# Four of sixteen query tiles as rounded products of split operands

## The chip, the cores and the metric

The kernel runs on one core of one Trainium2 chip. TensorE multiplies, VectorE and ScalarE work element by element, GpSimd and SyncE mostly issue DMA transfers. The metric is the time of one execution on the device in microseconds (us). The kernel before took 2002.85 us (median of three runs, 2001.03 to 2003.95).

## The reference, cut to what matters

One decoder layer for 256 prompt tokens and 8 sample tokens, 264 in all, with 2048 channels in float32: input projection, a recurrent and an attention group, output projection, layer norm, and then a retrieval of experts. The change lies at the start of that retrieval, in `q` and what follows from it:

```
q  = jnp.dot(xb, wq).reshape(n, PEER_HEADS, 2, PEER_HALF)      # 2048 x 2048 weights
s1 = jnp.einsum('nhd,hkd->nhk', q[:, :, 0], sub_k1)
s2 = jnp.einsum('nhd,hkd->nhk', q[:, :, 1], sub_k2)
v1, i1 = lax.top_k(s1, PEER_TOPK)
v2, i2 = lax.top_k(s2, PEER_TOPK)
comb = v1[..., :, None] + v2[..., None, :]
sv, si = lax.top_k(comb.reshape(n, PEER_HEADS, -1), PEER_TOPK)
e = take(i1, si // PEER_TOPK) * N_KEYS + take(i2, si % PEER_TOPK)
g = softmax(sv)
act = gelu(einsum(xb, u_tab[e]));  out = einsum(g * act, v_tab[e])
```

## The kernel before

**Two ways of multiplying.** A float32 matrix product is done in one of two ways. The native one (`native`, line 940) hands TensorE plain float32 operands. The rounded one splits both operands into a high part, rounded to the type float32r, and a low part, which is the rest, and adds three products: high by high, high by low, low by high. The weights are split on their way: `split1_` (lines 103 and 106) lets ScalarE copy the high half of a raw tile of 1024 columns, and VectorE subtract it from the raw tile. The split halves lie in a ring of five pairs of tiles; raw weights come by DMA, issued by SyncE, into a ring of six half tiles, so three tiles of weights are there or on their way.

**The query tiles.** After the first layer norm, `x1` (named M in the rows) holds 264 tokens as columns, in 16 chunks of 128 channels. There are 16 tiles of 128 query channels, counted m = 0 to 15, each a native product over the 16 chunks. Tiles 0 and 1 (`first`) run while the layer norm still finishes. From m = 2 on a loop issues, in this order: the load of the weights two tiles ahead, the product of tile m, for an even m the scores of head m/2 − 1 (`scores`), and the eviction of tile m (`queries`: a copy by ScalarE of 256 columns into qT, and one of 8 into QS).

**Scores and top 16.** `scores` multiplies the two query tiles of a head with its keys on TensorE; ScalarE copies the result into one of three tiles SC, and VectorE runs `both`: the 16 largest of each half, then the 16 largest sums. After every second head `pick` follows on VectorE, for both halves of the tokens.

**The split of x1.** The products that follow the query tiles are of the expert table and need only the first 214 tokens; they are mostly rounded and read `x1s`, the split of these 214 columns of `x1`. It is made in the loop, two chunks a tile, for m = 2 to 9, by one copy (ScalarE) and one subtraction (VectorE) a chunk.

**What sets the order.** Nothing is moved by a scheduler in this part: each engine takes its instructions in the order in which the program writes them, and waits at one that is not ready with everything behind it. Only DMA queues run apart. After the loop `early` issues tiles of the expert table, the last picks and the gates; from `GSTART` on, transposes on TensorE of what the picks and gates gave (`tokens`).

Of the kernel before, what the change touches and what calls it, by code (L numbers as in the profile page):

```python
# [10 lines left out]
F32R = mybir.dt.float32r  # L11
# [3 lines left out]
OP = mybir.AluOpType  # L15
# [3 lines left out]
NC_ = 16  # L19
SEQ = 256  # L20
NB = 8
T = SEQ + NB
NPG = 8
NG = 50
ND = T - NG
# [16 lines left out]
TABT = 20  # L42

RUN = 34
NAT = 6
PICK = 1
GATE = 3
# [13 lines left out]
def _build(tc, I, O):  # L61
    nc = tc.nc
    ctx = ExitStack()
    PS = bass.MemoryType.PSUM
    with ctx:
        def pool_in(c, name, bufs, side=None):
            return c.enter_context(tc.tile_pool(name=name, bufs=bufs, side=side, reuse_waits="tile"))

        const = pool_in(ctx, "const", 1)
        big = pool_in(ctx, "big", 1)  # L70
# [22 lines left out]
        def halves(src):  # L93
            return [half(src[:, a:a + 8]) for a in (0, 8)]
# [20 lines left out]
        def pmm(shape=(128, T)):  # L115
            return psum.tile(list(shape), F32, name="mm", bufs=mmb[0])
# [51 lines left out]
        for a in range(0, NC_, 4):  # L168
            for i, j in enumerate(seq[:3]):
                if a % 8 == 0:  # L170
                    first[j].append(slots[2 * i + a // 8]())
                hi, lo = [t[:, a % 8:a % 8 + 4] for t in first[j][-1]]
# [527 lines left out]
        x1, wo = x0, {}  # L700
# [24 lines left out]
        QS = x0w[:, :NB * 260]  # L725
# [47 lines left out]
        for u in range(2 * NC_):  # L773
# [3 lines left out]
            if u % 2 == 0:  # L777
# [3 lines left out]
                hi, lo = wo.pop(u // 2)  # L781
# [3 lines left out]
            p = pmm()  # L785
            for i in range(4):
                k, x = u % 2 * 4 + i, mixes[0][:, u // NC_ * 4 + i]
# [14 lines left out]
        def load_u(k):  # L802

            ups[k] = halves(I["wq"][k + 16] if k < 0 else I["uT"][k])

        def split1(d, k, i, eng=None):
            d[k][i] = split1_(d[k][i], eng)
# [11 lines left out]
        def split2(k, eng=None):  # L819
            split1(ups, k, 0, eng)  # L820
            split1(ups, k, 1, eng)
# [86 lines left out]
        for c in range(NC_ + 1):  # L908
# [5 lines left out]
            if c < NC_:  # L914
                p = pm[c] = pmm()
                w = [None, wo.pop(NC_ + c)]
# [16 lines left out]
        ln.squares(15)  # L933
        ln.stats(2)

        x1s = big.tile([128, NC_, 2, ND], F32R, name="A")
        first = [(ups.pop(k), pmm()) for k in (-16, -15)]

        def native(p, w, c, n=T):
            nc.tensor.matmul(p, w[c // 8][:, c % 8, :], x1[:, c, :n], start=c == 0, stop=c == NC_ - 1)  # L940
# [104 lines left out]
        QS = qp.tile([128, 16, 64], F32, name="QS", bufs=1)  # L1045
        nc.gpsimd.memset(QS, 0.0)
        qT = {}

        def queries(m, p):
            h = m // 2  # L1050
            if m % 2 == 0:
                qT[h] = qp.tile([128, 2, SEQ], F32, name="qT")
            nc.scalar.copy(qT[h][:, m % 2, :], p[:, :SEQ])
            nc.scalar.copy(QS[:, m, h * 8:(h + 1) * 8], p[:, SEQ:])

        def scores(h):
            q = qT.pop(h)
            ps = pmisc([128, 2, 2, 128])
            for tt in range(2):
                for f in range(2):  # L1060
                    nc.tensor.matmul(ps[:, tt, f, :], q[:, f, tt * 128:(tt + 1) * 128], kk[:, 2 * h + f, :],
                                     start=True, stop=True)
            sc = qp.tile([128, 2, 2, 128], F32, name="SC", bufs=3)
            nc.scalar.copy(sc, ps)
            both(tops, [sc[:, tt] for tt in range(2)], h)
            if h % 2 and h < 7:
                for t in tops:
                    t.pick(h - 1, 2)

        def rows_out(a):  # L1070

            p = pmisc([NG, 512])
            for c in range(4):
                nc.tensor.transpose(p[:, c * 128:(c + 1) * 128], x1[:, a * 4 + c, ND:T], ident)
            xg = qp.tile([NG, 512], F32, name="xg", bufs=1)
            nc.scalar.copy(xg, p)
            nc.gpsimd.dma_start(xgd[:, a * 512:(a + 1) * 512], xg)

        load_u(-13)
        for m, (w, p) in enumerate(first):  # L1080
            queries(m, p)
        for m in range(2, 16):
            k = m - 16
            load_u(k + 2)
            w = ups.pop(k)
            p = pmm()
            for i in range(NC_):
                native(p, w, i)
            if m % 2 == 0:
                scores(m // 2 - 1)  # L1090
            queries(m, p)
            if m < 10:

                for c in range(2 * (m - 2), 2 * (m - 2) + 2):
                    nc.scalar.copy(x1s[:, c, 0], x1[:, c, :ND])
                    nc.vector.tensor_tensor(x1s[:, c, 1], x1[:, c, :ND], x1s[:, c, 0], op=OP.subtract)
            elif m < 14:
                rows_out(m - 10)

        def sample_scores():  # L1100
# [86 lines left out]
        def load_v(k):  # L1187
            downs[k] = []
            for a in (0, 4):
                raw = stream.tile([128, 8, 128], F32, name="raw")  # L1190
                nc.sync.dma_start(raw, I["vt"][k][:, 2 * a:2 * a + 8])
                downs[k].append(raw)

        def up(k, a=0, b=NC_):
            w = ups[k]
            if a == 0:
                pu[k] = pmm([128, 2, ND])
            p = pu[k]
            if k < NAT:
                for c in range(a, b):  # L1200
                    native(p[:, 0], w, c, ND)
                return
            for c in range(a, b):
                hi, lo = w[c // 8]
                nc.tensor.matmul(p, hi[:, c % 8, :], x1s[:, c], start=c == 0, stop=False)  # L1205
                nc.tensor.matmul(p[:, 0, :], lo[:, c % 8, :], x1s[:, c, 0], start=False, stop=c == NC_ - 1)  # L1206

        def act_sum(k):
            p = pu.pop(k)
            acts[k] = ex.tile([128, NE], F32, name="ac", bufs=RUN - 8)  # L1210
            nc.gpsimd.memset(acts[k][:, ND:], 0.0)
            ac = acts[k][:, :ND]
            if k < NAT:
                nc.scalar.activation(ac, p[:, 0], AF.Gelu_apprx_tanh)
                return
            nc.scalar.copy(ac, p[:, 1, :])
            nc.vector.tensor_tensor(ac, ac, p[:, 0, :], op=OP.add)

        def act_gelu(k):
            if NAT <= k and k in acts:  # L1220
                ac = acts[k][:, :ND]
                nc.scalar.activation(ac, ac, AF.Gelu_apprx_tanh)
# [5 lines left out]
        def gate_mult(k):  # L1228
            g, i = divmod(k, 8)
            ac = acts[k]  # L1230
            nc.vector.tensor_tensor(ac.rearrange("p (b t) -> p b t", t=16), ac.rearrange("p (b t) -> p b t", t=16),  # L1231
                                    gts[g].rearrange("p (b i t) -> p b i t", i=8, t=16)[:, :, i, :], op=OP.mult)
            W[k] = epool[0].tile([128, 2, ND], F32R, name="w", bufs=17)
            nc.scalar.copy(W[k][:, 0], ac[:, :ND])  # L1234
# [24 lines left out]
        def step(s):  # L1259
            v = s - RUN  # L1260
            k = v + 9
            if s >= 128:
                return last_step(v, k)
            if s + 2 < 128:
                load_u(s + 2)
            if v >= -2:
                load_v(v + 2)
            if k + LEAD >= 0 and (k + LEAD) % 8 == 0:
                load_g((k + LEAD) // 8)
            up(s)  # L1270
            if v >= 0:
                split1(downs, v, 0)
                if v >= 1:
                    add(v - 1)
                split1(downs, v, 1)
            if s - 1 in pu:
                act_sum(s - 1)
            d, n = (ups, s + 1) if s + 1 < 128 else (downs, v + 1)
            high(d, n, 0)
            if k >= 0:  # L1280
                gate_mult(k)
            if s != RUN:
                act_gelu(s - 1)
            low(d, n, 0)
            if k >= 0:
                gate_low(k)
            split1(d, n, 1)
            if v >= 0:
                down(v)

        def last_step(v, k):
# [3 lines left out]
            for n in (v + 2, v + 3):  # L1295
                if n < 128 and n not in downs:
                    load_v(n)
            if v + RUN == 128:
                act_sum(127)
# [15 lines left out]
        def early(s, gen):  # L1315

            load_u(s + 2)
            if s + 1 >= NAT:
                split2(s + 1)
# [10 lines left out]
            if s == GATE:  # L1330
                for t in tops:
                    t.less()
                for t in tops:
                    t.gate()
            if NAT <= s < NAT + 8:
                for c in range(2 * (s - NAT), 2 * (s - NAT) + 2):

# [13 lines left out]
        gen = gates()  # L1351
        for s in range(GSTART, RUN - 9 - LEAD):
            early(s, gen)
# [3 lines left out]
        epool.append(pool_in(ctx, "exw", 2))  # L1357
        act_gelu(RUN - 12 - LEAD)
        act_gelu(RUN - 11 - LEAD)
# [224 lines left out]
```

## Time and profile before

| what | us |
|---|---|
| median of three runs | 2002.85 |
| lowest, highest | 2001.03, 2003.95 |
| the profiled execution: its time | 2001.45 |
| the profiled execution: its span | 1999.6 |
| TensorE busy in the span | 1931.7 (97%) |
| VectorE busy | 1623.9 (81%) |
| ScalarE busy | 964.2 (48%) |

All rows below come from the profiled execution; times in them count from the start of its span. "Busy" is the time in which an engine had an instruction under way. TensorE's matmuls overlap in its pipeline: the time between two starts, not the length of one, is what a matmul costs in a stream. A native float32 matmul shows as two records. The names on both sides of the arrow are the program's tiles: mm and misc lie in PSUM, A is `x1s`, hi, lo, xl and sometimes A are the halves of split weights, SC the score tiles, qT and QS the queries, sip, vp, combp, eqp, sfp, sap and r1p tiles of the top 16 and the picks.

### The profile page before, as it was taken

The numbers are of one execution on the slowest core, as the hardware profiler recorded it, in microseconds if no ns is written. First come the engines' busy times: TensorE is split into PE (matmuls) and PEld (weight loads), VectorE is DVE, ScalarE is ACT, GpSimd is POOL, SyncE is SP. The second block draws the span as 40 slices with busy tenths as digits, with TensorE's granted clock in tenths as the row PEclk, the third lists the DMA queues.
The fourth block names the chain that finished last, engine by engine and source line by source line (L and its number), as shares of the span: only waits on it lengthen the run. The fifth ranks groups of instructions, "written<-read, shape, count | busy, mean of one in ns | idle before, by whom it ended". The sixth has DMA issues, their size and how long they took to land.

```text
span 1999.6 us, 37148 instructions
## 1 busy us (share of the span) xinstructions
PE 1931.7 (97%) x13906; PEld 1834.9 (92%) x13906; DVE 1623.9 (81%) x2961; ACT 964.2 (48%) x1601; POOL 405.0 (20%) x461
## 2 busy tenths in 40 slices
PE   8999899999899999999999999999999999999995
PEld 8888778798789999999999999999999999999995
DVE  6534756785599889679999999899999996989977
ACT  4223655643211898555455445554455443544443
POOL 2000000004000000113333333233333330321012
PEclk9999999999999999999999999999999999999997
DMA  9899599854344578779999999899999995998851
GB/s 314 285 370 332 188 328 320 285 175 150 109 144 137 187 233 273 258 260 377 352 332 349 350 333 353 319 337 353 333 349 351 331 351 183 378 332 306 285 189 54
DMA packets 182260, 562.09 MB, mean 281 GB/s; under 512 B 20514, under 2 KB 49278, under 8 KB 181698
## 3 DMA queue, kind: packets, MB, share of 16 engines
q1 hardware_dynamic: 148656, 447.96, 63.1%
q0 software_dynamic: 32560, 111.70, 15.9%
q8 instruction: 109, 1.79, 0.4%
q14 instruction: 71, 0.58, 0.1%
q10 hardware_dynamic: 864, 0.06, 0.0%
HBM read 540.03 MB, written 19.61 MB: 280 GB/s over the span
## 4 chain that ended last, share of the span: by engine, by line
PE 82%; DVE 6%; DMA 6%; ACT 4%; issue 1%; SPq 1%; POOL 0%; POOLq 0%; ACTq 0%; DVEq 0%
PE acc L1249 21%; PE mm L1205 18%; PE acc L1251 10%; PE mm L1206 9%; PE mm L940 8%; PE mm L302 3%; PE mm L304 2%; PE mm L303 2%; DMA cv<-in_ck 2%; DMA cv<-in_cv 2%; DVE lo L106 1%; PE acc L1153 1%; PE acc L642 1%; PE acc L563 1%; PE misc L381 1%
## 5 line engine op out<-in xcount | busy, mean ns | idle before, releaser
L106 DVE TENSOR_TENSOR lo<-raw,hi 128x1024 fp32r<-128x1024 f32 x273 | 332.9, 1222 | 76.6 <-ACT hi L103 76.4
L1249 PE MATMUL acc<-w,hi 128*128 128x428 f32 x1224 | 387.2, 373 | 0.0
L1205 PE MATMUL mm<-A,hi 128*128 128x428 f32 x1176 | 369.2, 372 | 0.0
L103 ACT CAST hi<-raw 128x1024 fp32r<-128x1024 f32 x273 | 284.3, 1045 | 171.4 <-PE acc L1249 81.1
L1251 PE MATMUL acc<-w,lo 128*128 128x214 f32 x1224 | 321.0, 262 | 4.0 <-DVE lo L106 4.0
L1206 PE MATMUL mm<-A,lo 128*128 128x214 f32 x1176 | 308.0, 262 | 3.3 <-DVE lo L106 3.3
L1249 PE MATMUL acc<-w,xl 128*128 128x428 f32 x824 | 261.4, 371 | 0.0
L1205 PE MATMUL mm<-A,xl 128*128 128x428 f32 x776 | 242.6, 371 | 0.0
L1251 PEld LDWEIGHTS acc<-w,lo 128*128 128x128 f32 x1224 | 235.2, 192 | 4.4 <-DVE lo L106 4.3
L1249 PEld LDWEIGHTS acc<-w,hi 128*128 128x128 f32 x1224 | 231.3, 189 | 8.6
L1206 PEld LDWEIGHTS mm<-A,lo 128*128 128x128 f32 x1176 | 226.3, 192 | 3.6 <-DVE lo L106 3.6
L1205 PEld LDWEIGHTS mm<-A,hi 128*128 128x128 f32 x1176 | 222.4, 189 | 6.9
L1402 POOL DMA_INDIRECT ug<-in_u,eix x102 | 152.2, 1492 | 334.7 <-DVE ug L1420 254.9
L1251 PE MATMUL acc<-w,xl 128*128 128x214 f32 x824 | 216.4, 263 | 0.0
L1402 POOL DMA_INDIRECT ug<-in_v,eix x102 | 145.8, 1429 | 339.7 <-DVE xrep L1434 279.3
L1206 PE MATMUL mm<-A,xl 128*128 128x214 f32 x776 | 202.5, 261 | 0.0
L103 ACT CAST xl<-raw 128x1024 fp32r<-128x1024 f32 x139 | 143.2, 1046 | 101.3 <-PE acc L1249 81.4
L1257 DVE TENSOR_TENSOR M<-M,acc 128x428 f32<-128x428 f32 x256 | 153.5, 600 | 41.3 <-PE acc L1251 36.8
L106 DVE TENSOR_TENSOR xl<-raw,xl 128x1024 fp32r<-128x1024 f32 x139 | 170.5, 1229 | 15.3 <-ACT xl L103 15.3
L1234 ACT CAST w<-ac 128x214 fp32r<-128x214 f32 x128 | 47.7, 373 | 277.4 <-DVE ac L1231 277.4
L1249 PEld LDWEIGHTS acc<-w,xl 128*128 128x128 f32 x824 | 155.5, 189 | 5.6
L940 PE MATMUL mm<-M,raw 128*128 128x264 f32 (+1 forms) x704 | 152.8, 378 | 6.7 <-ACT M L901 6.7
(382 smaller groups left out, 4053.3 us busy)
## 6 DMA issues: line engine op xcount, KB each, us to landing
raw<-in_uT SPq DMA_DIRECT2D x256, 512.0 KB
raw<-in_vt SPq DMA_DIRECT2D x256, 512.0 KB
raw<-in_w_in SPq DMA_DIRECT2D x74, 512.0 KB
cv<-in_ck SPq DMA_DIRECT2D x64, 512.0 KB
cv<-in_cv SPq DMA_DIRECT2D x64, 512.0 KB
raw<-in_wq SPq DMA_DIRECT2D x32, 512.0 KB
Gd<-stage SPq DMA_DIRECT2D x14, 1024.0 KB
gt<-Gd SPq DMA_DIRECT2D x16, 896.0 KB
```

Source lines behind the costliest of these rows:

```text
L103: nc.scalar.copy(hi, raw)
L106: (eng or nc.vector).tensor_tensor(lo, raw, hi, op=OP.subtract)
L302: nc.tensor.matmul(p, hi, xh[:, c], start=c == 0, stop=False)
L303: nc.tensor.matmul(p, hi, xl[:, c], start=False, stop=False)
L940: nc.tensor.matmul(p, w[c // 8][:, c % 8, :], x1[:, c, :n], start=c == 0, stop=c == NC_ - 1)
L1205: nc.tensor.matmul(p, hi[:, c % 8, :], x1s[:, c], start=c == 0, stop=False)
L1206: nc.tensor.matmul(p[:, 0, :], lo[:, c % 8, :], x1s[:, c, 0], start=False, stop=c == NC_ - 1)
L1234: nc.scalar.copy(W[k][:, 0], ac[:, :ND])
L1249: nc.tensor.matmul(p[:, c, :2 * ND].rearrange("p (b t) -> p b t", b=2), hi[:, b % 8, :], w, start=i == 0, stop=False)
L1251: nc.tensor.matmul(p[:, c, :ND], lo[:, b % 8, :], w[:, 0], start=False, stop=i == 7)
L1257: nc.vector.tensor_tensor(a, a, p[:, :, b * ND:(b + 1) * ND], op=OP.add)
L1402: nc.gpsimd.indirect_dma_start(out=t, out_offset=None, in_=tab, in_offset=bass.IndirectOffsetOnAxis(ap=eix[:, a, j:j + 1], axis=0))
```

## The change

Tiles m = 4, 5, 6 and 7 (`QR`) become rounded products. Four things follow in the program:

- `x1s` now holds the high and the low part of all 264 tokens, 528 columns a chunk, in another order: high of the last 50 tokens, high of the first 214, low of the first 214, low of the last 50. So the 428 columns that the expert products read stay next to each other. `split_x1` makes it at m = 2, all 16 chunks at once, with two copies and two subtractions a chunk; the split in the loop is gone.
- At m = 3 to 6 the weights of the next tile are split (`split2`: two copies on ScalarE, two subtractions on VectorE) before the product of tile m is issued.
- Each of the four products writes 314 columns of PSUM: the first and third matmul of a chunk add into columns 0 to 263, the second (high weights by low tokens) into columns 50 to 313.
- The eviction of such a tile is three copies by ScalarE (214, 42 and 8 columns) and two additions by VectorE (42 and 8 columns), which bring the shifted parts together.

```diff
+QR = (4, 5, 6, 7)
...
-        x1s = big.tile([128, NC_, 2, ND], F32R, name="A")
+        x1s = big.tile([128, NC_, 2 * T], F32R, name="A")
+        LO = T
...
+            if m in QR:
+                a, b = qT[h][:, m % 2, :], QS[:, m, h * 8:(h + 1) * 8]
+                nc.scalar.copy(a[:, :ND], p[:, NG:T])
+                nc.scalar.copy(a[:, ND:], p[:, T:T + NG - NB])
+                nc.scalar.copy(b, p[:, T + NG - NB:T + NG])
+                nc.vector.tensor_tensor(a[:, ND:], a[:, ND:], p[:, :NG - NB], op=OP.add)
+                nc.vector.tensor_tensor(b, b, p[:, NG - NB:NG], op=OP.add)
+                return
             nc.scalar.copy(qT[h][:, m % 2, :], p[:, :SEQ])
             nc.scalar.copy(QS[:, m, h * 8:(h + 1) * 8], p[:, SEQ:])
...
+        def split_x1():
+            for c in range(NC_):
+                for a, b, t in ((0, NG, slice(ND, T)), (NG, T, slice(0, ND))):
+                    nc.scalar.copy(x1s[:, c, a:b], x1[:, c, t])
+                nc.vector.tensor_tensor(x1s[:, c, LO:LO + ND], x1[:, c, :ND], x1s[:, c, NG:T], op=OP.subtract)
+                nc.vector.tensor_tensor(x1s[:, c, LO + ND:], x1[:, c, ND:], x1s[:, c, :NG], op=OP.subtract)
...
-            p = pmm()
+            if m == 2:
+                split_x1()
+            if m + 1 in QR:
+                split2(k + 1)
+            p = pmm((128, T + NG) if m in QR else (128, T))
             for i in range(NC_):
-                native(p, w, i)
+                if m not in QR:
+                    native(p, w, i)
+                    continue
+                hi, lo = w[i // 8]
+                nc.tensor.matmul(p[:, :T], hi[:, i % 8, :], x1s[:, i, :T], start=i == 0, stop=False, ...)
+                nc.tensor.matmul(p[:, NG:], hi[:, i % 8, :], x1s[:, i, LO:], start=False, stop=False, ...)
+                nc.tensor.matmul(p[:, :T], lo[:, i % 8, :], x1s[:, i, :T], start=False, stop=i == NC_ - 1, ...)
             if m % 2 == 0:
                 scores(m // 2 - 1)
             queries(m, p)
-            if m < 10:
-                for c in range(2 * (m - 2), 2 * (m - 2) + 2):
-                    nc.scalar.copy(x1s[:, c, 0], x1[:, c, :ND])
-                    nc.vector.tensor_tensor(x1s[:, c, 1], x1[:, c, :ND], x1s[:, c, 0], op=OP.subtract)
-            elif m < 14:
+            if 10 <= m < 14:
                 rows_out(m - 10)
```

The expert products (`up`) read the same 428 columns of `x1s` under new indices.

What stands where now. First VectorE, between the end of the top 16 of scores 0 (MAX_INDEX sip) and the start of the top 16 of scores 1 (MAX vp of SC). Before:

```order
L975 MAX_INDEX sip_7112<-svp_7111,combp_7192 128x8
L975 MAX_INDEX sip_7118<-svp_7117,combp_7195 128x8
L1096 TENSOR_TENSOR A<-M,A 128x214 x4
L967 MAX vp_7269<-SC 128x8 x2
L967 MAX vp_7271<-SC 128x8 x2
```

and with the change, where `lo<-raw,hi` and `xl<-raw,xl` are the low halves of the weights of tiles 4 and 5:

```order
L978 MAX_INDEX sip_7112<-svp_7111,combp_7256 128x8
L978 MAX_INDEX sip_7118<-svp_7117,combp_7259 128x8
L107 TENSOR_TENSOR lo<-raw,hi 128x1024
L107 TENSOR_TENSOR xl<-raw,xl 128x1024 x2
L107 TENSOR_TENSOR lo<-raw,hi 128x1024
L970 MAX vp_7369<-SC 128x8 x2
L970 MAX vp_7371<-SC 128x8 x2
```

The subtractions of x1 have gone from here, and the low halves of two whole weight tiles stand between the two top 16.

Second VectorE, between the end of the picks after scores 1 (TENSOR_REDUCE r1p) and the top 16 of scores 2. Before:

```order
L1018 TENSOR_TENSOR eqp_7333<-eqp_7333,xfp_7116 128x512
L1019 TENSOR_REDUCE r1p_7121<-eqp_7333 128x32
L1096 TENSOR_TENSOR A<-M,A 128x214 x4
L967 MAX vp_7399<-SC 128x8 x2
L967 MAX vp_7401<-SC 128x8 x2
```

and with the change:

```order
L1021 TENSOR_TENSOR eqp_7433<-eqp_7433,xfp_7116 128x512
L1022 TENSOR_REDUCE r1p_7121<-eqp_7433 128x32
L1061 TENSOR_TENSOR qT<-qT,mm 128x42
L1062 TENSOR_TENSOR QS<-QS,mm 128x8
L107 TENSOR_TENSOR lo<-raw,hi 128x1024 x2
L1061 TENSOR_TENSOR qT<-qT,mm 128x42
L1062 TENSOR_TENSOR QS<-QS,mm 128x8
L107 TENSOR_TENSOR xl<-raw,xl 128x1024 x2
L970 MAX vp_7573<-SC 128x8 x2
L970 MAX vp_7575<-SC 128x8 x2
```

Behind the picks stand now the additions of tile 4 (qT, QS), the low halves of tile 6, the additions of tile 5 and the low halves of tile 7.

Third TensorE, from the end of tile 2 through scores 0 (misc from kk and qT). Before:

```order
L940 MATMUL mm<-M,raw 128x264 x48
L1061 MATMUL misc<-kk,qT 128x128 x4
L940 MATMUL mm<-M,raw 128x264 x32
L1061 MATMUL misc<-kk,qT 128x128 x4
L940 MATMUL mm<-M,raw 128x264 x32
```

and with the change:

```order
L943 MATMUL mm<-M,raw 128x264 x48
L1072 MATMUL misc<-kk,qT 128x128 x4
L943 MATMUL mm<-M,raw 128x264 x16
L1115 MATMUL mm<-A,hi 128x264
L1116 MATMUL mm<-A,hi 128x264
L1117 MATMUL mm<-A,lo 128x264
L1115 MATMUL mm<-A,hi 128x264
L1116 MATMUL mm<-A,hi 128x264
L1117 MATMUL mm<-A,lo 128x264
```

Tile 3 is native as before; tile 4 starts with two products of the high half, and its third matmul reads the low half `lo`, as does every third one behind it.

## Rows read from the trace of the kernel before

**Rows 1.** The page's busy times (us, share, instructions), then one of its groups.

```profile
PE 1931.7 (97%) x13906; PEld 1834.9 (92%) x13906; DVE 1623.9 (81%) x2961; ACT 964.2 (48%) x1601; POOL 405.0 (20%) x461
...
L103 ACT CAST hi<-raw 128x1024 fp32r<-128x1024 f32 x273 | 284.3, 1045 | 171.4 <-PE acc L1249 81.1
```

**Rows 2.** Windows: length, busy time by engine (instructions), granted clock, DMA share, GB/s.

```profile
545.00:575.00 30.00, 30.00 (x145) 25.89 (x144) 29.20 (x130) 4.62 (x19) 0.00 (x0) 1.00 0.42 140
...
575.00:605.00 30.00, 30.00 (x145) 25.77 (x144) 29.45 (x132) 4.76 (x16) 1.08 (x2) 1.00 0.46 147
...
700.00:750.00 50.00, 48.01 (x357) 46.64 (x356) 44.14 (x114) 46.85 (x111) 1.42 (x10) 1.00 0.75 233
...
750.00:800.00 50.00, 46.69 (x343) 45.82 (x342) 45.67 (x130) 41.73 (x87) 0.00 (x0) 0.99 0.87 274
```

**Rows 3.** TensorE's timeline of the query tiles: start, us, engine, line, operation, records.

```profile
529.31 14.41 PE L940 MATMUL mm<-M,raw 128*128 128x264 f32 x64
...
543.55 1.05 PE L1061 MATMUL misc<-kk,qT 128*128 128x128 f32 x8
...
544.44 14.41 PE L940 MATMUL mm<-M,raw 128*128 128x264 f32 x64
...
573.82 1.05 PE L1061 MATMUL misc<-kk,qT 128*128 128x128 f32 x8
```

**Rows 4.** VectorE's timeline there; in brackets the idle time before, and its end.

```profile
530.13 0.87 DVE L967 MAX8 vp<-SC 128x8 f32<-128x128 f32 x4 [16.97 <-ACT SC L1064]
...
539.33 1.23 DVE L1096 TENSOR_TENSOR A<-M,A 128x214 fp32r<-128x214 f32 x4
...
545.26 0.87 DVE L967 MAX8 vp<-SC 128x8 f32<-128x128 f32 x4 [4.70 <-ACT SC L1064]
...
564.35 1.25 DVE L1096 TENSOR_TENSOR A<-M,A 128x214 fp32r<-128x214 f32 x4
```

**Rows 5.** TensorE's timeline of an input projection tile, three products a chunk.

```profile
19.72 0.28 PE L302 MATMUL mm<-xh,A 128*128 128x264 f32 x1
...
22.86 0.29 PE L304 MATMUL mm<-xh,lo 128*128 128x264 f32 x1
```

**Rows 6.** VectorE's timeline: the low halves of one weight tile.

```profile
665.63 1.23 DVE L106 TENSOR_TENSOR lo<-raw,hi 128x1024 fp32r<-128x1024 f32 x1 [1.18 <-ACT hi L103]
...
666.78 1.22 DVE L106 TENSOR_TENSOR xl<-raw,xl 128x1024 fp32r<-128x1024 f32 x1
```

**Rows 7.** ScalarE's timeline of the query tiles.

```profile
521.32 0.17 ACT L1054 COPY QS<-mm 128x8 f32<-128x8 f32 x1
...
521.50 0.37 ACT L1053 COPY qT<-mm 128x256 f32<-128x256 f32 x1
...
529.51 0.59 ACT L1064 COPY SC<-misc 128x512 f32<-128x512 f32 x1 [7.57 <-PE misc L1061]
...
530.31 0.66 ACT L1095 CAST A<-M 128x214 fp32r<-128x214 f32 x2
```

**Rows 8.** TensorE behind a wait: its timeline, then windows (busy, granted clock, DMA).

```profile
399.70 0.56 PE L788 MATMUL mm<-A,hi 128*128 128x264 f32 x1 [1.94 <-ACT A L281]
...
400.06 0.43 PE L789 MATMUL mm<-A,hi 128*128 128x264 f32 x1
...
402.26 0.42 PE L790 MATMUL mm<-A,lo 128*128 128x264 f32 x1
...
400.00:401.00 1.00, 1.00 (x6) 0.50 0.70 278
...
403.00:404.00 1.00, 1.00 (x10) 0.98 0.63 172
```

**Rows 9.** VectorE's last gate, and TensorE's first token transpose.

```profile
657.55 0.29 DVE L1032 TENSOR_TENSOR gp<-gp,zsp 128x128 f32<-128x128 f32 x1
...
659.75 0.27 PE L1115 MATMUL misc<-c_ident,r0p 128*128 128x128 f32 x1
```

**Rows 10.** VectorE's timeline: an operation on 32 columns.

```profile
554.47 0.15 DVE L1011 TENSOR_SCALAR sap<-sip 128x32 uint32<-128x32 uint32 x1
```

More of the change, by code (lines that the diff above doesn't have):

```diff
@@ L1085, in _build @@
             w = ups.pop(k)
-            p = pmm()
-            for i in range(NC_):
-                native(p, w, i)
+            if m == 2:
[3 more added lines that the diff above has]
+            p = pmm((128, T + NG) if m in QR else (128, T))
+            for i in range(NC_):
+                if m not in QR:
+                    native(p, w, i)
+                    continue
+                hi, lo = w[i // 8]
+                nc.tensor.matmul(p[:, :T], hi[:, i % 8, :], x1s[:, i, :T], start=i == 0, stop=False, skip_group_check=True)
+                nc.tensor.matmul(p[:, NG:], hi[:, i % 8, :], x1s[:, i, LO:], start=False, stop=False, skip_group_check=True)
+                nc.tensor.matmul(p[:, :T], lo[:, i % 8, :], x1s[:, i, :T], start=False, stop=i == NC_ - 1,
+                                 skip_group_check=True)
             if m % 2 == 0:
@@ L1204, in up @@
                 hi, lo = w[c // 8]
-                nc.tensor.matmul(p, hi[:, c % 8, :], x1s[:, c], start=c == 0, stop=False)
-                nc.tensor.matmul(p[:, 0, :], lo[:, c % 8, :], x1s[:, c, 0], start=False, stop=c == NC_ - 1)
+                nc.tensor.matmul(p, hi[:, c % 8, :], x1s[:, c, NG:NG + 2 * ND].rearrange("p (b t) -> p b t", b=2), start=c == 0, stop=False)
+                nc.tensor.matmul(p[:, 0, :], lo[:, c % 8, :], x1s[:, c, NG:T], start=False, stop=c == NC_ - 1)
         def act_sum(k):
```

## The prediction

> **What bounds the kernel now.** I read the busy times first, then a table of windows around the query tiles, then the timelines of TensorE, VectorE and ScalarE there. TensorE is busy 97% of the span and VectorE 81% [rows 1]; such a share hides which stage is whose. The windows show it: from 545 to 575 us TensorE is busy for all 30.00 us, and VectorE for 29.20 of them [rows 2]. So TensorE sets the pace while the query tiles run, but VectorE has almost nothing left there. Two query tiles without the scores between them take 14.24 us on TensorE (529.31 to 543.55), 7.12 each, and the scores 0.89 [rows 3]. Below, tile m is the m-th of the 16, counted from 0; "query tiles 5 to 8" are m = 4 to 7, and scores h follow the product of tile 2h+2. Scores 3 begin at 573.82 [rows 3]: that is the mark against which I compare.
>
> On VectorE the two top-16 stages of one head take from 530.13 to 539.33, 9.20 us. After scores 1 the picks follow: 545.26 to 564.35, 19.09 us [rows 4]. Today no product of this stage reads anything that VectorE writes; TensorE needs of it only that one of three score tiles in SBUF is free, so VectorE may lag. The change gives TensorE a new need.
>
> **The products.** A native tile is 16 matmuls in 7.12 us. A rounded one is 48 matmuls of 264 columns; 26 steps of such a stream went from 19.72 to 22.86, 0.1208 us a step [rows 5], so a tile takes 5.80 us. That is 1.32 saved per tile, 5.3 us in four, if TensorE never waits. The Trainium skill (TensorE: Matmul & The Clock Gate, section Back-to-back issue gap) gives N/2.4 + 2.5 ns for an isolated warm matmul, 112.5 ns for 264 columns; an estimate by that page makes a tile 5.4 us and the four tiles 1.6 us shorter again. The measured stream is of the same shape and operands' type, so it decides.
>
> **Splitting x1.** ScalarE's 32 casts now stand behind the evictions of tiles 0 and 1, which end about 521.9. 214 columns step by about 0.29 (two in 0.66 with 0.37 for the last), and 8 columns by 0.18 [rows 7]; 50 lie between, 0.20 taken. 16 pairs are 7.8 us and end at 529.7. The copy of scores 0 starts at 529.51 today [rows 7], so it is late by 0.2 (0 to 1.5 by the two bounds). VectorE's 32 subtractions run beside the casts, in a wait of 16.97 us [rows 4], so they cost nothing; the 16 that stood in the stage before (four in 1.23 [rows 4], 4.9 us in all) are gone from it.
>
> **Splitting the weights.** Four tiles need two casts each on ScalarE, 1.045 us on the mean [rows 1]; ScalarE is busy for 4.62 of 30 us in this stage [rows 2], so they hide. They also need two subtractions each on VectorE, which step by 1.15 [rows 6]: 2.3 us a tile, 9.2 in all. These do not hide, because of where they stand in VectorE's queue: those of tiles 4 and 5 behind the top-16 of scores 0, and those of tile 6 behind the top-16 and the picks of scores 1. TensorE's third matmul of such a tile already reads the low half. Behind it on TensorE wait the rest of the tile, the next scores and all later tiles. DMA loads of later weights wait for buffers that these splits free, but run a tile and more ahead of TensorE, at a DMA share of 0.42 [rows 2]; hidden. The eight pairs of halves come out of a ring of five; a pair's last reader, the tile two before, is done by then.
>
> **Evictions.** Three copies for two on ScalarE: hidden. On VectorE two additions a tile from PSUM, 42 and 8 columns: no such row stands in the trace; the nearest are 0.15 for 32 columns [rows 10] and 0.31 for 214 [rows 4]. I take 0.17 each, 0.35 a tile; by the bounds 0.3 to 0.6.
>
> **The new chain, step by step.**
> 1. Tile 3 ends at 529.31 + 7.12 = 536.43. Top-16 of scores 0 ends at 539.5 (0.2 late), the first subtraction of tile 4 at 540.8. TensorE has done two matmuls (0.24) and waits 4.1 us.
> 2. The 46 left take 5.56: 546.4, and 547.9 with the clock (below).
> 3. From scores 1 to the first MAX8 on VectorE is 545.26 − 543.55 = 1.71 [rows 3, 4]: 549.6. VectorE has been free since 544.1.
> 4. Top-16 and picks, 19.09: 568.7. Additions of tile 4, 0.35, first subtraction of tile 6, 1.2: 570.25.
> 5. TensorE did scores 1 and tile 5 meanwhile: 547.9 + 0.89 + 5.80 = 554.6. With two matmuls of tile 6 done it waits 15.4 us.
> 6. Tile 6: 570.25 + 5.56 + 1.5 = 577.3. Scores 2, tile 7 (split by 573), native tile 8: 0.9 + 5.80 + 7.12. Scores 3 begin at 591.1, for 573.82 before: 17.3 us late.
>
> **The clock.** At 399.70 TensorE came back from a wait of 1.94 us; the granted clock had gone to 0.50, the 1.2 GHz level, and was back at 0.98 in the window from 403. Between 400.06 and 402.26 products of 264 columns stepped by 0.22 instead of 0.1208 [rows 8, 5]. Over 3.3 us of work that loses 3.3 × (1 − 0.1208/0.22) = 1.5 us. Both new waits are longer, so I charge 1.5 twice, 3.0 (0 to 4.5 as bounds). The Trainium skill (the same page, section HAM oscillation) puts the loss at the throttled time times one half, 1.65 us each; by that page the sum would be 0.3 us more.
>
> **Sum.** −5.3 saved, +4.1 and +15.4 waited, +3.0 clock: +17.2, the 17.3 of the chain but for rounding. After scores 3 the order is that of before, and VectorE starts the next top-16 without arrears. Later the token transposes at 659.75 need gates that VectorE finished at 657.84 [rows 9], 1.9 us of slack. Both hang on scores 7, before which VectorE waited for its scores, so both move alike. From there TensorE works as before. The profiled execution took 2001.45, 1.40 less than the median 2002.85; 2001.45 + 17.3 = 2018.7, and against the median 2020.1. I forecast **2020**. With the bounds (clock 0 to 4.5, additions, casts up to 1.5 late) this case alone reaches 2017 to 2023.
>
> **Rivals.**
> A. *VectorE keeps up* (the other side). If the low halves were ready when TensorE arrives, only the saving is left: 2002.85 − 5.3 = 1997.6. It would decide if the subtractions of tile 6 ended before 549, but 19.09 us of top-16 and picks stand ahead of them. 3%.
> B. *The waits stay, the clock does not fall.* Then the chain is 3.0 us shorter: +14.3, 2017.1. Against it: the row after 1.94 us of idling. For it: the first wait is short. 14%.
> C. *Part is won back later.* From 700 to 800 us TensorE idles 1.99 + 3.31 us [rows 2]; if it arrives later and VectorE not, these shrink: at most 5.3 back, 2014.8. Against it: VectorE's later work hangs on the same late scores. 6%.
> D. *VectorE is later than I think after scores 3.* It carries 9.2 + 1.4 − 4.9 = 5.7 us more; if its waits don't take that up, the transposes wait for 5.7 − 1.9 = 3.8 us: 2024. 8%.
> E. *No change*: all of it absorbed by a stage that something else paces. I see none: the longest pause of TensorE in the rows behind is 3.31 us of 50 [rows 2]. 3%.
>
> **How the numbers follow.** The forecast has 66%, B 14, C 6, D 8, A 3, E 3. Leaving about 10% on each side at most, the range is 2013 to 2025. A difference under 0.2% (4 us) can't be told from no change: faster 3% (A), same 3% (E), slower 94%.
>
> **What would show it.** In the profile of the changed kernel: a wait of the third product of tile 4 on VectorE's low half of about 4 us, one of about 15 at tile 6, none at tiles 5 and 7; granted clock 0.50 behind each; VectorE without a pause between scores 1 and the subtractions of tile 6; scores 3 some 17 us later; all stages after 600 us moved by that, with unchanged lengths. If tile 6 doesn't wait, the forecast is wrong at its main step; if tile 6 waits but the end moves by less than 10 us, the claim that everything behind follows is wrong.

## The result, and the profile after

The changed kernel takes 2020.15 us (median of four executions, 2017.22 to 2323.98), the kernel before 2003.40. One of the four had a mean granted clock of 0.747 and is left out of the ratio, which is **1.009, 95% interval 1.0064 to 1.0115**: 18 us slower, by 13 to 23. The forecast was 2020, in a range of 2013 to 2025. The profiled execution took 2019.94 us, with a span of 2018.2.

The busy line of its page (share of the span, number of instructions) answers to [rows 1]:

```profile
PE 1932.4 (96%) x13970; PEld 1836.5 (91%) x13970; DVE 1636.7 (81%) x2993; ACT 976.1 (48%) x1629; POOL 405.4 (20%) x461
```

The shares hardly moved, so the difference has to be found by stages. TensorE's timeline around the query tiles (start, length, line, operation, tiles and shapes, number; in brackets idle time and what ended it) answers to [rows 3]:

```profile
501.92 0.81 PE L943 MATMUL mm<-M,raw 128*128 128x264 f32 x1 [6.75 <-ACT M L902]
...
525.24 1.05 PE L1072 MATMUL misc<-kk,qT 128*128 128x128 f32 x8
526.13 7.29 PE L943 MATMUL mm<-M,raw 128*128 128x264 f32 x32
...
537.41 0.59 PE L1117 MATMUL mm<-A,lo 128*128 128x264 f32 x1 [3.75 <-DVE lo L107]
537.80 0.42 PE L1115 MATMUL mm<-A,hi 128*128 128x264 f32 x1
538.02 0.42 PE L1116 MATMUL mm<-A,hi 128*128 128x264 f32 x1
...
545.73 1.05 PE L1072 MATMUL misc<-kk,qT 128*128 128x128 f32 x8
...
568.00 0.59 PE L1117 MATMUL mm<-A,lo 128*128 128x264 f32 x1 [15.12 <-DVE lo L107]
...
576.38 1.05 PE L1072 MATMUL misc<-kk,qT 128*128 128x128 f32 x8
...
651.19 1.05 PE L1072 MATMUL misc<-kk,qT 128*128 128x128 f32 x8
...
676.17 0.27 PE L1140 MATMUL misc<-c_ident,r0p 128*128 128x128 f32 x1
```

The third product of tile 4 waits for its low half, and so does that of tile 6; those of tiles 5 and 7 do not. The first row is the last wait of the kernel's earlier part, which the change does not touch.

VectorE in the same stretch answers to [rows 4]:

```profile
526.95 0.87 DVE L970 MAX8 vp<-SC 128x8 f32<-128x128 f32 x4 [1.06 <-ACT SC L1075]
...
536.13 1.23 DVE L107 TENSOR_TENSOR lo<-raw,hi 128x1024 fp32r<-128x1024 f32 x1
...
547.44 0.87 DVE L970 MAX8 vp<-SC 128x8 f32<-128x128 f32 x4 [6.68 <-ACT SC L1075]
...
565.95 0.69 DVE L1022 TENSOR_REDUCE r1p<-eqp 128x32 f32<-128x512 f32 x1
566.55 0.19 DVE L1061 TENSOR_TENSOR qT<-qT,mm 128x42 f32<-128x42 f32 x1
566.65 0.15 DVE L1062 TENSOR_TENSOR QS<-QS,mm 128x8 f32<-128x8 f32 x1
566.73 2.35 DVE L107 TENSOR_TENSOR lo<-raw,hi 128x1024 fp32r<-128x1024 f32 x2
```

From 547.44 to 566.73 VectorE does the top-16 of scores 1, the picks and two additions without a pause, and only then the low halves of tile 6, for which TensorE has waited since 552.88 (568.00 − 15.12).

The windows of the same kernel (busy time of the engines, then the granted clock, the share of the DMA engines and GB/s) answer to [rows 2] and [rows 8]:

```profile
core 0: us, PE busy (x) PEld busy (x) DVE busy (x) ACT busy (x) POOL busy (x), PEclk, DMA share, GB/s
536.00:537.00 1.00, 0.00 (x0) 0.00 (x0) 1.00 (x2) 0.00 (x0) 0.00 (x0) 0.72 0.11 41
537.00:543.00 6.00, 5.59 (x25) 5.59 (x26) 3.76 (x4) 0.00 (x0) 0.00 (x0) 0.50 0.72 203
543.00:544.00 1.00, 1.00 (x9) 1.00 (x8) 0.00 (x0) 0.00 (x0) 0.00 (x0) 0.87 0.85 221
556.00:567.00 11.00, 0.00 (x0) 0.00 (x0) 10.45 (x26) 0.00 (x0) 0.00 (x0) 0.54 0.00 0
568.00:573.00 5.00, 5.00 (x22) 5.00 (x23) 3.53 (x5) 0.00 (x0) 0.00 (x0) 0.50 0.77 235
573.00:574.00 1.00, 1.00 (x6) 1.00 (x6) 0.00 (x0) 0.00 (x0) 0.00 (x0) 0.51 0.79 152
574.00:575.00 1.00, 1.00 (x10) 1.00 (x9) 0.00 (x0) 0.00 (x0) 0.00 (x0) 1.00 0.78 234
```

Behind each wait the clock is 0.50, the 1.2 GHz level, until about 543.3 and 574.0, worked out from the windows in which it rises (0.87 and 0.51).

The span divides at marks that every kernel of this study has: W, the return from TensorE's last wait before the query tiles; S0, S3 and S7, the starts of scores 0, 3 and 7; T, the first token transpose. In us, from the starts in the traces (scores 3 begin at 590.24 in the changed kernel):

| stretch | before | before, second profile | changed | difference to the first |
|---|---|---|---|---|
| start to W | 505.12 | 502.57 | 501.92 | −3.20 |
| W to S0 | 23.29 | 23.53 | 23.32 | +0.03 |
| S0 to S3 (tiles 3 to 8) | 45.40 | 45.40 | 65.00 | **+19.60** |
| S3 to S7 | 60.95 | 60.95 | 60.95 | 0 |
| S7 to T | 24.98 | 24.98 | 24.98 | 0 |
| T to the end | 1339.88 | 1337.84 | 1342.01 | +2.13 |

The sum is +18.56, the difference of the spans. The start to W can't come from the change: its code is the same in both, and over all 14 profiles here (only e8 changes its code) it scatters from 501.92 to 512.40. So single executions must be compared by stages, and whole times by ratios.

### The profile page after: what moved, and what is told of

It reads as the page before. It is cut to its first block, busy times and chain, and to the rows that moved or that the text cites. A ratio compares the mean times of both kernels' runs of the same rounds, so it can differ in the third digit from the quotient of the medians.

```text
span 2018.2 us, 37349 instructions
## 1 busy us (share of the span) xinstructions
PE 1932.4 (96%) x13970; PEld 1836.5 (91%) x13970; DVE 1636.7 (81%) x2993; ACT 976.1 (48%) x1629; POOL 405.4 (20%) x461
## 4 chain that ended last, share of the span: by engine, by line
PE 79%; DVE 9%; DMA 5%; ACT 4%; issue 2%; SPq 1%; POOL 0%; POOLq 0%; DVEq 0%; ACTq 0%
PE acc L1274 20%; PE mm L1230 18%; PE acc L1276 10%; PE mm L1231 9%; PE mm L943 6%; PE mm L303 3%; PE mm L305 2%; PE mm L304 2%; DVE lo L107 2%; DMA cv<-in_ck 2%; DMA cv<-in_cv 1%; PE acc L1178 1%; PE acc L564 1%; PE acc L643 1%; DMA raw<-in_uT 1%
## 5 line engine op out<-in xcount | busy, mean ns | idle before, releaser
L107 DVE TENSOR_TENSOR lo<-raw,hi 128x1024 fp32r<-128x1024 f32 x278 | 338.6, 1222 | 76.5 <-ACT hi L104 75.3
L104 ACT CAST xl<-raw 128x1024 fp32r<-128x1024 f32 x142 | 148.3, 1049 | 100.9 <-PE acc L1274 41.9
L107 DVE TENSOR_TENSOR xl<-raw,xl 128x1024 fp32r<-128x1024 f32 x142 | 174.2, 1230 | 17.3 <-ACT xl L104 17.2
L1276 PEld LDWEIGHTS acc<-w,xl 128*128 128x128 f32 x824 | 158.0, 192 | 7.0 <-DVE xl L107 6.9
L1274 PEld LDWEIGHTS acc<-w,xl 128*128 128x128 f32 x824 | 155.5, 189 | 5.7
```

The costliest lines, as they stand in the source:

```text
L104: nc.scalar.copy(hi, raw)
L107: (eng or nc.vector).tensor_tensor(lo, raw, hi, op=OP.subtract)
L1274: nc.tensor.matmul(p[:, c, :2 * ND].rearrange("p (b t) -> p b t", b=2), hi[:, b % 8, :], w, start=i == 0, stop=False)
L1276: nc.tensor.matmul(p[:, c, :ND], lo[:, b % 8, :], w[:, 0], start=False, stop=i == 7)
```

## The experiments

The low halves, the picks and the additions all stand in VectorE's queue. The rivals asked: is it the low halves alone; is the clock a cost of its own; does the new operand cost something by itself? The expectations of e1 to e8 count the stage from the start of tile 3, 0.89 us behind S0, so 0.89 goes off the values of S0 to S3 below before the two are compared. Ratios are to the kernel before, run beside each variant.

**One tile at a time.** Tile 5 has its low halves in time, tile 6 has not.

```diff
-QR = (4, 5, 6, 7)
+QR = (5,)          # e1; (6,) in e2
```

> Only tile 5 is a rounded product (QR = (5,)); everything else is as in the change. The stage is measured from the start of tile 3 to the start of scores 3: 44.5 us before, 64.1 with the change. Theory of order (the price is the place of the low halves in VectorE's queue): those of tile 5 are issued before scores 1 and stand behind the top 16 of scores 0 alone, which end well before TensorE gets there; no wait, no fall of the clock, stage 43.2 us, end about 1.3 us earlier than before, which the timing can hardly tell from none. Theory of work (a rounded tile costs VectorE and the evictions what they have not got, wherever it stands): a quarter of the change's loss, stage about 49 us, end 4 to 5 us later than before.

> Only tile 6 is a rounded product (QR = (6,)); the same work as with tile 5 alone, one tile later. Theory of order: its low halves stand behind the top 16 and the picks of scores 1 (19.1 us), so TensorE waits about 13.8 us at its third matmul, then runs 26 products at half clock (2.6 us); stage 44.5 - 1.3 + 13.8 + 2.6 = 59.6 us, end 15 us later than before (ratio 1.0075). Theory of work: the same as with tile 5 alone, 4 to 5 us later than before.

Tile 5 alone: ratio 1.0054 (1.0033 to 1.0075), S0 to S3 52.15 us; tile 6 alone: 1.0107 (1.0082 to 1.0131), 60.27 us. From the start of tile 3 that is 51.26 and 59.38. The wait at tile 6 was foreseen (59.6); at tile 5 neither theory was right (43.2 and about 49), and the saving did not come. TensorE's and VectorE's timelines of the kernel with tile 5 alone say why:

```profile
561.08 0.83 PE L1072 MATMUL misc<-kk,qT 128*128 128x128 f32 x6
568.28 0.79 PE L1072 MATMUL misc<-kk,qT 128*128 128x128 f32 x2 [6.37 <-DVE qT L1061]
```
```profile
567.44 0.69 DVE L1022 TENSOR_REDUCE r1p<-eqp 128x32 f32<-128x512 f32 x1
568.04 0.19 DVE L1061 TENSOR_TENSOR qT<-qT,mm 128x42 f32<-128x42 f32 x1
568.14 0.15 DVE L1062 TENSOR_TENSOR QS<-QS,mm 128x8 f32<-128x8 f32 x1
```

No low half is late. It is the addition from PSUM, 0.19 us of work, that stands behind the picks of scores 1, and scores 2 read what it writes. In the changed kernel this wait is covered: tile 6 waits in front of scores 2 for the same picks. The row of tile 6 alone shows that one wait, and no other in the stage (its whole time came out 21 us longer, 6 more than the stage; in its profile 5.7 of them lie behind T, and what made them is not known):

```profile
567.76 0.59 PE L1117 MATMUL mm<-A,lo 128*128 128x264 f32 x1 [13.66 <-DVE lo L107]
```

**The low halves taken off VectorE.** In e3 ScalarE makes a second rounded copy in place of the difference, so the low part of the weights' split is left out of these products; in e7 GpSimd subtracts.

```diff
-                split2(k + 1)
+                for n in (0, 1):
+                    raw = ups[k + 1][n]
+                    hi, lo = slots[next(turn_) % len(slots)]()
+                    nc.scalar.copy(hi, raw)
+                    nc.scalar.copy(lo, raw)
+                    ups[k + 1][n] = (hi, lo)
```
```diff
-                split2(k + 1)
+                split2(k + 1, nc.gpsimd)
```

> The change, but the low halves of the weights of tiles 4 to 7 are written by a second copy on ScalarE instead of a subtraction on VectorE (the output of these products is then not the reference's: the low part is left out of it). Theory of order: both waits go, nothing falls to half clock; four tiles at 5.8 us; stage 7.1 + 23.2 + 1.8 + 7.1 = 39.2 us, end 5.3 us earlier than before (ratio 0.9974). If products, evictions or the moved split of x1 had a part in the loss, it stays: stage over 44.5.

> The change, but the subtractions of the low halves of tiles 4 to 7 run on GpSimd. By the trace GpSimd takes 0.97 to 1.61 us for 264 columns, so 3.8 to 6.2 for 1024. Theory of order: the long wait at tile 6 goes and short waits at each tile come in its place; worked through tile by tile the stage is 42 us at 3.8 and 62 us at 6.2 us a half (44.5 before, 64.1 with the change). If the queue of VectorE were not the cause, it would stay at 64 or more whatever GpSimd takes.

e3: ratio 1.0026 (1.0014 to 1.0039), S0 to S3 49.84 us. e7: 1.0055 (1.0036 to 1.0074), 52.66 us. In neither does a product wait for a low half, and in both the wait reappears at scores 2; TensorE's rows of e3 and of e7:

```profile
560.59 1.22 PE L1072 MATMUL misc<-kk,qT 128*128 128x128 f32 x4 [7.87 <-DVE qT L1061]
```
```profile
563.22 1.22 PE L1072 MATMUL misc<-kk,qT 128*128 128x128 f32 x4 [10.08 <-DVE qT L1061]
```

So most of the time comes back with the low halves gone from VectorE, but not the change of sign that was expected of e3: the low halves are not the only thing behind the picks. GpSimd took 2.37 us a half, less than the 3.8 to 6.2 expected of it.

**The picks moved.** The picks of scores 1 are issued behind the eviction of tile 7.

```diff
-            if h % 2 and h < 7:
+            if h % 2 and 1 < h < 7:
...
             queries(m, p)
+            if m == 7:
+                for t in tops:
+                    t.pick(0, 2)
```

> The change, but the picks that follow scores 1 (9.9 us of VectorE) are issued behind tile 7's eviction instead. Theory of order: the low halves of tile 6 stand behind the top 16 of scores 1 alone; the wait at tile 6 falls from 15.1 to 5.2 us, half clock follows it still, stage 64.1 - 9.9 = 54.2 us; VectorE makes up for the picks before the transposes. End about 9 us later than before (ratio 1.0045). Theory of work: VectorE has the same to do, the stage stays at 64.

Ratio 1.0055 (1.0036 to 1.0075); S0 to S3 55.04 us, 9.95 less than in the changed kernel. That is the picks' own length: 19.09 for top-16 and picks less 9.20 for the top-16 is 9.89 [rows 4]. The wait at tile 4 stays at 3.75, that at tile 6 falls from 15.12 to 5.22, the rest of the top-16. S7 to T stays 24.98, so the picks are not missed later:

```profile
538.08 0.59 PE L1117 MATMUL mm<-A,lo 128*128 128x264 f32 x1 [3.75 <-DVE lo L107]
...
558.82 0.59 PE L1117 MATMUL mm<-A,lo 128*128 128x264 f32 x1 [5.22 <-DVE lo L107]
```

**The waits filled.** TensorE does 28 and 120 products whose result nothing reads, ahead of tiles 4 and 6. The low halves come as late as in the changed kernel (12.17 us behind the start of scores 0, 22.28 for 22.27 behind that of scores 1), but TensorE idles for only 0.34 and 0.53 us.

```diff
+            if m in (4, 6):
+                fill = pmisc([128, T])
+                for _ in range(28 if m == 4 else 120):
+                    nc.tensor.matmul(fill, w[0][0][:, 0, :], x1s[:, 0, :T], start=True, stop=True)
```

> The change, but TensorE runs 28 products of 264 columns into an unread PSUM tile before tile 4 and 120 before tile 6 (3.4 and 14.5 us at full clock), so that it works through its two waits of 3.75 and 15.1 us. Theory with the clock: no window at 0.50 there, the 52 products that ran at 0.22 us run at 0.121, stage 64.1 - 5.2 = 58.9 us, end about 14 us later than before (ratio 1.007). If the slow products have another cause than idling: stage still 64.

Ratio 1.0084 (1.0058 to 1.0111); S0 to S3 59.75 us, **5.25 less** than without the filling. Its timeline and its windows show the two waits down to their ends and the clock at 1.00 throughout:

```profile
545.84 0.39 PE L1121 MATMUL mm<-A,lo 128*128 128x264 f32 x1 [0.34 <-DVE lo L107]
...
573.83 0.40 PE L1121 MATMUL mm<-A,lo 128*128 128x264 f32 x1 [0.53 <-DVE lo L107]
```
```profile
545.00:552.00 7.00, 6.66 (x56) 6.45 (x54) 4.19 (x4) 0.00 (x0) 0.00 (x0) 1.00 0.56 174
556.00:568.00 12.00, 12.00 (x101) 12.00 (x100) 11.66 (x46) 2.39 (x5) 0.00 (x0) 1.00 0.01 1
573.00:580.00 7.00, 6.47 (x53) 6.25 (x52) 4.37 (x6) 0.00 (x0) 0.00 (x0) 1.00 0.66 174
```

The clock is thus a cost of its own, and larger than forecast. This is read from the stage; the whole times, 1.0084 and 1.009, can't tell the two kernels apart.

**Other tiles.** Tiles 2, 3 and 5, with x1 split ahead of the first evictions, and the first weights split earlier.

```diff
-QR = (4, 5, 6, 7)
+QR = (2, 3, 5)
...
         ln.stats(2)
+        high(ups, -14, 0)
+        high(ups, -14, 1)
...
         load_u(-13)
+        low(ups, -14, 0)
+        low(ups, -14, 1)
+        split_x1()
         for m, (w, p) in enumerate(first):
...
-            if m == 2:
-                split_x1()
```

> Tiles 2, 3 and 5 rounded instead of 4 to 7; x1 is split before the evictions of tiles 0 and 1, the high half of tile 2's weights during the layer norm, its low half behind the norm's centering. All low halves then stand before a top 16 that is not yet due. Theory of order: no wait, three tiles at 5.8 us, 4.0 us saved, 1.2 us of VectorE work a pair of tiles gone from the loop; end 4 us earlier than before (ratio 0.998), at the edge of what five rounds can tell. If ScalarE or VectorE is late for tiles 2 and 3: waits of 1 to 3 us each, no change against before. Theory of work: later than before by 4 us or more.

Ratio 1.0045 (1.0030 to 1.0060). S0 to S1 is 13.85 us for 15.13 before, which is the saving of one tile; at tile 5 the wait of the kernel with that tile alone comes back, 6.35 us of scores 2 for the addition. So the gain expected of these three tiles (0.998) was lost, at that step and in the slow products behind it.

**The split alone, and where its parts stand.** No rounded query tile, only the split of all 264 tokens (e6); the same with the whole operand shifted by 14 elements (e9); the same with both parts of the 214 tokens at the start of the row (e12, of which only the reads are shown; the split writes there too).

```diff
-QR = (4, 5, 6, 7)
+QR = ()
```
```diff
-        x1s = big.tile([128, NC_, 2 * T], F32R, name="A")
+        x1a = big.tile([128, 14 + NC_ * 2 * T], F32R, name="A")
+        x1s = x1a[:, 14:].rearrange("p (c t) -> p c t", c=NC_)
```
```diff
-x1s[:, c, NG:NG + 2 * ND]   x1s[:, c, NG:T]
+x1s[:, c, :2 * ND]          x1s[:, c, :ND]
```

> QR = (): all query tiles native, but x1 is split at m = 2, all 264 tokens, in the new order of columns. Theory of order: the split lies in VectorE's and ScalarE's idle time; stage 44.5 us, end as before within 1 us (ratio 1.000). If the moved split holds up the copy of scores 0 or the expert products read the new order slower, the end is later by 1.5 us or more.

> The new split alone (no rounded query tiles), with the whole split operand shifted by 14 elements, so that the part of the 214 tokens starts at byte 256 of its row instead of byte 200. In all variants with the new operand the 214-column up product of the late stage steps by 99.7 ns (97.6 before), about 1950 times. Theory 'start of the operand': the step goes back to 97.6 ns (98.0 at most) and the stretch from the token transposes to the end is 3 to 4 us shorter than with the split alone; time over that of before 1.0000 (0.999 to 1.001). Rival 'row length' (2112 bytes from chunk to chunk, 1712 before): the step stays at 99.7 ns and the ratio at 1.001 to 1.002.

> The kernel before, profiled once more. If the later differences are the change's and not this one execution's: the 214-column up product steps by 97.6 ns, and from the token transposes (first of the three after scores 7) to the end it takes 1339.9 us within 1 us, with a wait of about 4.0 us of TensorE on VectorE's low half about 1700 us. Rival 'scatter of the profile': 1342 to 1344 us and a wait of 5 to 6 us, as in the variants.

> The new split alone, its rows still 2112 bytes from chunk to chunk, but with both parts of the 214 tokens at the start of the row, as in the kernel before (there a row has 1712 bytes). Means of steps in the late stage, 428 and then 214 columns: before 207.55 and 97.60 ns; with the split alone (start at byte 200) 207.23 and 99.71; shifted (byte 256) 208.48 and 97.85. Theory 'start in the row alone': 207.5 and 97.6, the pair back at 305.2 ns, and the last 7000 to the last 2000 matmuls take 764.5 us as before. Rival 'row length': with a start at a multiple of 64 bytes the pair stays at 306.3 ns as in the shifted one, 766.3 us. Rival 'neither': the pair stays at 306.9. Time over before: 1.000 to 1.002 in each case.

Ratios: e6 1.0011 (1.0000 to 1.0022), e9 1.0025 (1.0007 to 1.0043), e12 1.0020 (1.0006 to 1.0034). These can't be told from each other. In all three S0 to S3 is 45.40 us, as before: the split costs nothing in its own stage. What it costs lies in the late up products, which read the same operand. Means of the steps from start to start between 830 and 1640 us, some 1300 of each:

| kernel | the 214 tokens start at | row | 428 columns, ns | 214 columns, ns | pair, ns |
|---|---|---|---|---|---|
| before, and e10 | byte 0 | 1712 bytes | 207.55 | 97.60 and 97.61 | 305.15 |
| changed, e1, e3 to e8 | 200 | 2112 | 207.21 to 207.25 | 99.71 to 99.76 | 306.94 to 306.98 |
| e9 (e11 within 0.03) | 256 | 2112 | 208.48 | 97.85 | 306.33 |
| e12 | 0 | 2112 | 208.53 | 97.77 | 306.30 |

(In e2 one wait lies among these steps.) The theory of the start alone is refuted: with the start at byte 0 the pair is still 1.15 ns longer than before. The new row length goes with 1.15 ns of the 1.8; the odd start makes the long product 1.3 ns shorter and the short one 1.9 longer, 0.65 in all. There are 1952 such pairs (1176 and 776 by the lines of the profile), so 1.81 ns make 3.5 us by this reckoning. The pairs of the last products (acc from w), which read another operand, kept theirs: 306.44 ns before, 306.42 in the changed kernel. Why a longer row costs a nanosecond was not tried.

The second profile of the kernel before (e10, one execution, 1997.10 us) was to show whether the later difference is scatter. TensorE's return from its last two long waits, in the first profile, the second and the changed kernel:

```profile
799.18 0.55 PE L1206 MATMUL mm<-A,lo 128*128 128x214 f32 x1 [3.31 <-DVE lo L106]
...
1700.43 0.55 PE L1251 MATMUL acc<-w,lo 128*128 128x214 f32 x1 [3.99 <-DVE lo L106]
```
```profile
797.25 0.55 PE L1206 MATMUL mm<-A,lo 128*128 128x214 f32 x1 [3.31 <-DVE lo L106]
...
1699.21 0.55 PE L1251 MATMUL acc<-w,lo 128*128 128x214 f32 x1 [4.77 <-DVE lo L106]
```
```profile
815.75 0.36 PE L1231 MATMUL mm<-A,lo 128*128 128x214 f32 x1 [3.23 <-DVE lo L107]
...
1719.90 0.55 PE L1276 MATMUL acc<-w,xl 128*128 128x214 f32 x1 [5.70 <-DVE xl L107]
```

Between them lie 901.25, 901.96 and 904.15 us. The wait at 1700 varies by itself (4.0 and 4.8 before, 4.9 to 6.3 in all kernels with the new operand), and what lengthens it stays open. Without the wait the stretch takes 897.26, 897.20 and 898.45 us, 1.2 longer where its 1567 pairs make 2.8; but in both profiles of before the clock falls once more ahead of that wait (at 1679.6 and 1677.5, for 3.4 us), and in the changed kernel it does not. So the 3.5 us stand by themselves in no stretch. Of what was expected of e10 the step came (97.61 ns), but neither the wait of 4.0 nor the 1339.9 us from T to the end. From T to the end the two profiles of before have 1339.9 and 1337.8 us, the twelve with the new operand 1339.5 to 1345.6, on the mean 1342.1: the longer end is likely, but two profiles of before don't fix its size.

**Three moves together.** GpSimd's low halves (e7), the later picks (e5) and the shift (e9).

> The change with three moves: GpSimd subtracts the low halves of the query tiles' weights, the picks of scores 1 stand behind the eviction of tile 7, and the split operand is shifted by 14 elements. Theory (VectorE's queue is all that costs): no wait of TensorE on low halves or on additions between tile 3 and scores 3, granted clock 1.00 there, scores 0 to scores 3 take 40.1 us (45.4 before, 65.0 changed); scores 7 to the transposes stay 25.0. Ratio 0.9975 to 0.999. Rival 'VectorE is the bound next': scores 3 come as early, but the gates are late and the stretch from scores 7 to the transposes grows from 25.0 to 26 to 29 us; ratio 0.999 to 1.001. Rival 'additions still late': scores 2 or 3 wait for the additions from PSUM by 3 us or more, ratio above 1.001.

Ratio to the kernel before **0.9987 (0.9975 to 0.9998)**, against 1.009 for the change as it was: 1998.22 us, the only one here that is faster than the kernel before, by 0.02 to 0.25%. TensorE waits for nothing from S0 to T:

```profile
530.21 1.05 PE L1073 MATMUL misc<-kk,qT 128*128 128x128 f32 x8
531.10 7.29 PE L944 MATMUL mm<-M,raw 128*128 128x264 f32 x32
...
544.20 1.05 PE L1073 MATMUL misc<-kk,qT 128*128 128x128 f32 x8
...
556.95 1.05 PE L1073 MATMUL misc<-kk,qT 128*128 128x128 f32 x8
```

S0 to S3 is 40.67 us (scores 3 at 570.88; 40.1 was expected), 4.73 less than before, and S7 to T stays 24.98. So the saving is real once VectorE's queue is out of its way. That removing low halves alone (e7, 52.66) or picks alone (e5, 55.04) is not enough while both together give 40.67 shows that two needs of TensorE, the low halves and the additions, stood behind the same work of VectorE. The third move has no part in this stage: in e9 it is 45.40 us.

## Why the prediction was right, and which terms were off

By its steps, with the values of the changed kernel:

| term | predicted | measured |
|---|---|---|
| four rounded tiles | −5.3 | −5.1 (step 121.8 ns in place of 120.8) |
| wait at tile 4 | +4.1 | +3.9 (3.75 idle) |
| wait at tile 6 | +15.4 | +15.3 (15.12 idle) |
| clock | +3.0 (0 to 4.5) | +5.0 |
| first product behind each wait | none | +0.5 (0.39 for 0.12 us, twice) |
| S0 to S3 | +17.3 | +19.60 |
| T to the end | 0 | +2.1 and +4.2 (by the two profiles of before) |

The profile counts idle time from the end of a product (0.28 us long), the prediction from the end of its step (0.12 us), hence the two values of a wait.

**The main step** held: the low halves stand behind the top-16 of scores 0 and, at tile 6, behind top-16 and picks of scores 1. Its working could be made before the run because all durations on VectorE's queue were there in rows of before, and because the top-16 follows its scores at a fixed distance (1.71 us in both traces). Tiles 5 and 7 did not wait, as forecast, and S3 to T moved unchanged to a hundredth of a microsecond, which refutes rival D. C foresaw shorter waits between 700 and 800 us: the longest of them is still 3.23 us for 3.31 (the rows at 815.75 and 799.18 above), and T to the end grew. A and E fall by the ratio, and B by the windows.

**The step that was mis-sized** is the clock, "I charge 1.5 twice, 3.0 (0 to 4.5 as bounds)". The row it came from had the low clock for 3.3 us of work behind a wait of 1.94 us [rows 8]. Here it stayed low for 5.9 and 6.0 us behind the waits of 3.75 and 15.12: 51 steps of 219 ns on the mean instead of 121.8 make 5.0 us, beside the first product of each. The filled waits give 5.25 by subtraction; 0.3 of it is the first products', which step by 0.23 us there. 5.0 and 5.25 both lie outside the bound. The Trainium skill (TensorE: Matmul & The Clock Gate, section HAM oscillation) takes half of the time spent at the low clock as the loss, 5.9 us of the 11.9 here; steps and first products make 5.5. The rule was good, and what was missing was the length of the low stretch.

More rows of the same profile would have widened the bound. Behind its waits of 3.31, 3.99 and 6.75 us (returns at 799.18, 1700.43 and 505.12) the clock was low for 3.2, 3.1 and 3.7 us of work, but behind those of 2.61 and 2.93 (237.82 and 1974.49) for 4.8 and 5.5. The last return, and windows behind it (columns as above):

```profile
1974.49 1.25 PE L847 MATMUL misc<-ug,ones 128*128 128x264 f32 x2 [2.93 <-POOL ug L845]
```
```profile
1974.50:1979.00 4.50, 4.50 (x10) 3.52 (x11) 1.20 (x3) 0.77 (x2) 0.00 (x0) 0.50 0.00 0
1979.00:1980.00 1.00, 1.00 (x4) 0.74 (x3) 0.00 (x0) 0.00 (x0) 0.00 (x0) 0.50 0.00 0
1980.00:1981.00 1.00, 1.00 (x5) 0.54 (x3) 0.38 (x1) 0.00 (x0) 0.00 (x0) 1.00 0.00 0
```

The variants show as much, and no order by the length of the wait: 6.0 and 5.8 us behind 3.75 and 5.22 (e5), 2.9 behind 6.37 (e1), 3.1 behind 7.87 (e3), 4.4 behind 10.08 (e7), 5.0 behind 13.66 (e2). Windows of e1 behind its return at 568.28:

```profile
568.00:571.00 3.00, 2.72 (x7) 2.27 (x8) 1.57 (x11) 0.93 (x3) 0.00 (x0) 0.50 0.00 0
571.00:572.00 1.00, 1.00 (x6) 0.80 (x4) 1.00 (x9) 0.00 (x0) 0.00 (x0) 0.93 0.00 0
```

**"From there TensorE works as before"** failed by a little: the up products read the operand that the change lays out anew, and each pair became 1.8 ns longer. The prediction followed instructions and waits, not the addresses of an operand that other stages share.

**A need that was priced but not followed** is the addition from PSUM. It was counted as 0.35 us of work a tile (its two operations take 0.18 together by their starts), but not as a wait of scores 2. The wait at tile 6 covered this; e1, e3, e7 and e8 uncovered it. ScalarE's casts, bounded by 1.5 us, cost nothing: x1's 32 casts ended at 525.27, and the copy of scores 0 began at 526.33, 1.09 us behind the start of its scores (1.10 before).

That 2020 met the median is in part luck: the stage came out 2.3 us longer and the end 2 to 4 us, and in the two profiles compared here a start 3.2 us shorter, which the change does not touch, took most of that back. The measured ratio, 18 us with an interval of 10, can't tell 17.3 from 22.

## What to carry to other kernels

Before moving work to a faster form on one engine, list every new read that this engine gets from another, and look what stands ahead of each in that engine's queue; here 0.2 us of additions behind top 16 and picks held TensorE up for 6.4 to 10.1 us, the low halves for 15.1, and mending one only uncovered the other. Charge the half clock for as long as waits in the trace show it, and take the bounds from several such rows; those of the kernel before had 3.1 to 5.5 us of work at it, and a longer wait was not followed by a longer stretch. When an operand is laid out anew, find its other readers and multiply even a nanosecond by their number.

## What the runs showed of the hardware

- A product's step depends slightly on where its moving operand lies: 214 columns took 97.6 to 97.9 ns with a start at byte 0 or 256 of the row and 99.7 at byte 200, while 428 columns went the other way in rows of 2112 bytes, 208.5 ns against 207.2.
- GpSimd subtracts halves of 128x1024 in 2.37 us, next to 1.22 to 1.24 on VectorE; beside TensorE's pace of 5.8 us a tile, which takes two of them, that was fast enough. The two rows of GpSimd in e11 are those of tile 4:

```profile
533.25 2.37 POOL L107 TENSOR_TENSOR lo<-raw,hi 128x1024 fp32r<-128x1024 f32 x1 [40.22 <-ACT hi L104]
535.58 2.40 POOL L107 TENSOR_TENSOR xl<-raw,xl 128x1024 fp32r<-128x1024 f32 x1
```

- Behind the waits named above, of 1.94 to 15.12 us, the granted clock stayed at 0.50 for 2.9 to 6.0 us of work, with no order by the length of the wait; around one of 3.22 us in e3 (return at 800.92) it stayed at 1.00.
- The stretch ahead of the query tiles, the same code in all profiles but that of e8, took 501.92 to 512.40 us, which is more scatter than from T to the end (1339.5 to 1345.6 with the new operand).
